# Order of the first loads, the norm of the input and the last root in a two-layer trunk on one core

## The chip, the cores and the metric

The kernel runs on one core of one Trainium2 chip. The metric is the device time of one execution in microseconds (us), the median of several runs. Engines are called by short names: PE is TensorE's matmul, PEld its weight load, DVE is VectorE, ACT is ScalarE, POOL is GpSimd, SP is SyncE, whose queue (SPq) issues nearly all loads.

## The reference, cut to what matters

Two layers over x, 256 tokens of 2048 features in float32. Layer 0 has a mixer of a convolution branch and an attention branch, layer 1 a gated recurrence; each mixer is followed by a gated feed-forward block. Ahead of each of the four blocks, and once at the end, stands this norm:

```
def rmsnorm(x, w):
    xf = x.astype(jnp.float32)
    y = xf * lax.rsqrt(jnp.mean(xf * xf, axis=-1, keepdims=True) + EPS)
    return (y * w.astype(jnp.float32)).astype(x.dtype)

h = rmsnorm(x, norm_w[layer, 0])
u = h @ w_in                       # layer 0: the first matmuls of the kernel
a, g = jnp.split(u[..., :2048], 2, axis=-1)
h = a * jax.nn.sigmoid(g)          # then the convolution over tokens
```

The last line of the trunk is `rmsnorm(x, final_norm_w)`.

## The kernel before, in words

**Precision.** Every large product is made from a high part and a low part of each factor (`fp32r`). `split` (L130) makes them for activations: ACT writes the high part (L138), DVE the low part (L139). `units` (L173) makes them for weights: it loads a raw tile (L184, three buffers), and for each unit of 128x1024 ACT writes the high part `whi` (L198) and DVE or POOL the low part `wlo` (L199; `lo_pool` says how many of four go to POOL). These two are traced with a raised priority (300).

**Norm by postponement.** The factor 1/rms of a token is not needed before a matmul. x goes in scaled by the norm's weight alone, and the product is multiplied by 1/rms afterwards, in the step that empties an accumulator. `norm_done` (L367) sums the squares, `inv_rms` (L152) takes the root (`rsqrt`, L141: a first guess from the bits and three rounds of three instructions), puts it on a diagonal (`rs_diag`, L162, two instructions) and broadcasts it with one matmul (L166); ACT copies the result to `rs_bc` (L168).

**The first layer's start.** x lies in memory twice, by features (`in_x`, for the matmuls) and by tokens (`in_xt`, for the squares). `run` (L1289) loads the small table `cst_a`, warms PE up with 12 products of ones (L1303), and `first_norm(i)` (L1308) loads a quarter of `in_x` in two halves and splits it. `even` (L422) then drives chunks of 256 columns of the input weights, one job each: 16 steps of 128 features, four units of four steps, 24 matmuls in a unit (L224 to L226), two accumulators. Chunk 0 is a gate chunk: `evac_g` multiplies the accumulator by `rs_bc` and takes the sigmoid; chunk 1 is its value chunk: `evac_a` multiplies it by that gate into `cin`, from which the convolution (L463 to L473, on DVE) starts. There are four accumulator banks (`ps_acc`), so two chunks can be in the making. In the text the units are numbered through: 0 to 3 are those of chunk 0 (each with a raw tile of its own, 512 KB), 4 to 7 those of chunk 1 (two raw tiles of 1 MB).

**What sets the order.** `drive` (L281) runs the jobs step by step and traces the background steps it is given between them, spread over the share `until` of the steps. A planner then orders each engine's instructions, by priority and by its own reckoning of when operands are there; on the chip each engine follows that order. In chunk 0 the background steps are the quarters 1 and 2 of x and `first_sums` (L1318), which takes quarter 3, the load of `in_xt` (2 MB), eight squares on ACT (L1326) and `norm_done`. In chunk 1 it is the load of the large table `cst_b` (838 KB).

**The end.** The last block's last column block is made one half of the tokens after the other (`half_job`, L261). `last` (L1342) adds the squares of each of four column blocks; with the last one it sums the four, takes the root with `rsqrt` and scales and stores the result. For the second half of the tokens this chain ends the kernel.

Of the kernel before, what the change touches and what calls it, by code (L numbers as in the profile page):

```python
# [10 lines left out]
F32 = mybir.dt.float32  # L11
F32R = mybir.dt.float32r
I32 = mybir.dt.int32
U8 = mybir.dt.uint8
AF = mybir.ActivationFunctionType
ALU = mybir.AluOpType
AX = mybir.AxisListType

S = 256
D = 2048  # L20
# [4 lines left out]
EPS = 1e-6  # L25
# [42 lines left out]
class Net:  # L68
# [58 lines left out]
    def quarter(self, tag, shape=(128, 4, 2, S), dtype=F32R):  # L127
        return self.tile(self.act, list(shape), tag, dtype, bufs=1)

    def split(self, dst, src, scale=None):  # L130

        nc = self.nc
        hi, lo = dst[:, 0, :], dst[:, 1, :]
        if scale is None:
            nc.scalar.activation(hi, src, AF.Copy)
            nc.vector.tensor_sub(lo, src, hi.bitcast(F32))
        else:
            nc.scalar.activation(hi, src, AF.Copy, scale=scale)  # L138
            nc.vector.scalar_tensor_tensor(lo, src, scale, hi.bitcast(F32), op0=ALU.mult, op1=ALU.subtract)  # L139
# [279 lines left out]

    def even(self, xhl, start):  # L422
        nc, a = self.nc, self.a
        ep_ctx, cv_ctx, ns_ctx = ExitStack(), ExitStack(), ExitStack()
        ep = self.ep = ep_ctx.enter_context(self.tc.tile_pool(name="ep", bufs=1))
# [9 lines left out]
        def scaled(ps):  # L435
            u = self.t256("e_u")
            nc.vector.tensor_mul(u, ps[:, :S], self.bc)
            return u

        def job(c, evac):  # L440
            return (8, self.w_job(wi[c], KD, xhl, evac, joint=True))

        def evac_g(i):
            def f(nt, ps):
                g = self.t256("f_g", bufs=4)
                nc.scalar.activation(g, scaled(ps), AF.Sigmoid)
                nc.gpsimd.tensor_mul(g, g, self.bc)
                gates[2 * i + nt] = g

            return f  # L450

        def evac_a(i):
            def f(nt, ps):
                j = 2 * i + nt
                nc.vector.tensor_mul(cin[:, j, PAD:], ps[:, :S], gates[j])

            return f
# [25 lines left out]
        def ln_steps():  # L483
            st = {}
            w, b = self.cb("lnw"), self.cb("lnb")
            four = lambda t: t.unsqueeze(1).to_broadcast([128, 4, S])

            def mean(j0, j1):
                if j0 == 0:
                    st["m"] = self.mx()[:, :S]  # L490
                for j in range(j0, j1):
                    nc.tensor.matmul(st["m"], self.mean1024, cy[:, j], start=(j == 0), stop=(j == 7))

            def center(h):
                y = cy[:, 4 * h : 4 * h + 4]
                nc.vector.tensor_sub(y, y, four(st["m"]))
                q = st[h] = self.quarter(f"mhl{h}", (128, 4, S), F32)
                nc.scalar.activation(q, y, AF.Square)

            def var():  # L500
                v = self.mx()[:, :S]
                for j in range(8):
                    nc.tensor.matmul(v, self.mean1024, st[j // 4][:, j % 4], start=(j == 0), stop=(j == 7))
                st["v"] = self.t256("rs_diag", bufs=1)
                nc.vector.tensor_scalar(st["v"], v, EPS, None, op0=ALU.add)
                st["r"] = self.t256("rs_bc", bufs=2)

            def root():
                self.rsqrt(st["r"], st["v"], "ln")

            def out(h):
                y = cy[:, 4 * h : 4 * h + 4]
                nc.vector.tensor_mul(y, y, four(st["r"]))
                for j in range(4 * h, 4 * h + 4):
                    nc.scalar.activation(cy[:, j], cy[:, j], AF.Silu, scale=w[:, j : j + 1], bias=b[:, j : j + 1])

            def parts(h):
                y = cy[:, 4 * h : 4 * h + 4]
                self.mhl(4 * h)
                q = self.mhl.have[h]  # L520
                nc.scalar.activation(q[:, :, 0, :], y, AF.Copy)
                nc.vector.tensor_sub(q[:, :, 1, :], y, q[:, :, 0, :].bitcast(F32))

            two = lambda f: [lambda: f(0), lambda: f(1)]
            rest = [self.rest]
            return [lambda: mean(0, 6)], (
                [lambda: mean(6, 8)] + two(center) + rest * 2 + [var, root] + two(out) + rest + two(parts)
            )
# [47 lines left out]
        def evac_c(kv):  # L576
# [9 lines left out]


        self.raw_size = 1024
        self.drive([job(0, evac_g(0))], start, until=0.75)
        self.raw_size = 2048  # L590
        self.lo_pool = (0, 1, 1, 1)
        ln_first, ln_rest = ln_steps()
        self.drive([job(1, evac_a(0))], [lambda: nc.sync.dma_start(self.cst_b, a["cst_b"])], until=0.25)
        self.drive(
            conv_job(1)
            + conv_job(2)
# [6 lines left out]
            until=0.98,  # L603
# [6 lines left out]
            until=0.8,  # L610
# [3 lines left out]
        sums = []  # L614
# [30 lines left out]
        for i in range(11):  # L645
            for late, k in ((3, "values"), (2, "turn0"), (2, "turn1"), (1, "weigh"), (0, "scores0"), (0, "scores1")):
                if 0 <= i - late < 8:
                    P, j = divmod(i - late, 4)
# [640 lines left out]
    def run(self):  # L1289
        nc, a = self.nc, self.a  # L1290
        self.cst_a = self.tile(self.fix, [128, NA], "cst_a")
        self.cst_b = self.tile(self.fix, [128, NB], "cst_b")
        nc.sync.dma_start(self.cst_a, a["cst_a"])
        self.x = self.tile(self.fix, [128, 2, D], "x")
        self.ones = self.tile(self.fix, [128, 128], "ones")
        nc.vector.memset(self.ones, 1.0)
        self.mean1024 = self.tile(self.fix, [128, 128], "mean1024")
        nc.vector.memset(self.mean1024, 1.0 / 1024)


        warm = self.mx()
        for _ in range(12):
            nc.tensor.matmul(warm[:, 0:128], self.ones, self.ones, start=True, stop=True)  # L1303

        xhl = self.new_xhl()
        xw = []

        def first_norm(i):  # L1308

            xw.append(self.quarter(f"mhl{i}", (128, 2, 4, S), F32))  # L1310
            for h in range(2):
                x = xw[i][:, 0, 2 * h : 2 * h + 2]
                nc.sync.dma_start(x, a["x"][:, i * 4 + 2 * h : i * 4 + 2 * h + 2, :])
            for j in range(4):
                f = 4 * i + j
                self.split(xhl(f), xw[i][:, 0, j], self.nw(0)[:, f : f + 1])

        def first_sums():  # L1318
            first_norm(3)
            nc.sync.dma_start(self.x, a["xt"])  # L1320
            self.ss = self.tile(self.tp, [128, 2, 4], "n_ss", bufs=2)
            with self.tc.high_priority(offset=-60):
                for tb in range(2):
                    for c in range(4):
                        junk = xw[c][:, 1].rearrange("p a b -> p (a b)")[:, tb * 512 : tb * 512 + 512]
                        nc.scalar.activation(  # L1326
                            junk, self.x[:, tb, c * 512 : c * 512 + 512], AF.Square, accum_out=self.ss[:, tb, c : c + 1]
                        )
            self.norm_done()

        first_norm(0)
        xhl = self.even(xhl, [lambda: first_norm(1), lambda: first_norm(2), first_sums])

        nxt = self.new_xhl()
        self.ffn(a["gu0"], a["dn0"], xhl, self.to_norm(self.nw(2), nxt))
        xhl = self.odd(nxt)

        fw = self.ctx.enter_context(self.tc.tile_pool(name="fw", bufs=1))
        fnw = self.tile(fw, [128, D], "fnw")
        nc.sync.dma_start(fnw, a["fnw"])  # L1340

        def last(c, tb):  # L1342

            self.square(c, tb)
            cols = [slice(i * 512, i * 512 + 512) for i in range(4)]
            x = [self.x[:, tb, i] for i in cols]
            if c < 3:
                nc.gpsimd.tensor_mul(x[c], x[c], fnw[:, cols[c]])
                return
            v = self.tile(self.tp, [128, 1], "l_v", bufs=2)  # L1350
            nc.vector.tensor_reduce(out=v, in_=self.ss[:, tb], op=ALU.add, axis=AX.X)
            nc.vector.tensor_scalar(v, v, 1.0 / D, EPS, op0=ALU.mult, op1=ALU.add)
            r = self.tile(self.tp, [128, 1], "l_r", bufs=2)
            self.rsqrt(r, v, "l")
            for i in (0, 1, 2, 3):
                if i == 3:
                    nc.vector.scalar_tensor_tensor(x[i], x[i], r, fnw[:, cols[i]], op0=ALU.mult, op1=ALU.mult)
                elif i == 0:
                    nc.vector.tensor_scalar(x[i], x[i], r, None, op0=ALU.mult)
                else:  # L1360
                    nc.scalar.activation(x[i], x[i], AF.Copy, scale=r)
                nc.sync.dma_start(a["out"][:, tb, cols[i]], x[i])

        self.ffn(a["gu1"], a["dn1"], xhl, last, keep=fw)


# [108 lines left out]
```

## Time and profile before

| | us |
|---|---|
| median of 3 runs | 2377.88 (2377.82 to 2378.31) |
| the profiled execution's own time | 2373.59 |
| span of its profile (first to last instruction) | 2371.8 |
| PE busy in it | 2350.5 |
| PE's mean granted clock | 0.997 of full |

The profile is that of one execution. Busy times don't tell how fast a matmul goes: PE counts as busy at either clock. The granted clock is given as a share of 2.4 GHz, so 0.50 is 1.2 GHz. In a row of a time line the first number is the start, the second the time from there to the end, both in us; "x4" merges four instructions; what stands in brackets is the engine's idle time just before and what ended it.

### The profile page before, as it was taken

To read this page: it belongs to the slowest core of one execution; us is meant where nothing else is said; L and a number is where in the kernel's file an instruction comes from. 1 tells how busy PE (TensorE), PEld (TensorE's weight loads), DVE (VectorE), ACT (ScalarE), POOL (GpSimd) and SP (SyncE) were. 2 spreads that over 40 slices of the span, in tenths; PEclk is the share of its full clock that TensorE was granted. 3 is DMA by queue.
4 is the path that set the end of the run, shared out by engine and by line. 5 is a ranking of instruction groups with operands and counts; after the bars stand their busy time and mean duration, and the time that the engine had idled before them with its cause. 6 is when DMAs were issued, how large, how long until landed. Compare 5 with 4: busy or idle time off the path is not lost.

```text
span 2371.8 us, 33574 instructions
## 1 busy us (share of the span) xinstructions
PE 2350.5 (99%) x13318; PEld 2026.6 (85%) x13318; DVE 1483.3 (63%) x2251; ACT 1144.2 (48%) x1648; POOL 401.7 (17%) x420
## 2 busy tenths in 40 slices
PE   8999999999999999999999999999999999999998
PEld 8999878888888888888888888888888888888886
DVE  5997677655555555555657777756555555555655
ACT  5345666554345434445544444445554344434443
POOL 4651311111011101110113333300110011101111
PEclk9999999999999999999999999999999999999999
DMA  7555534555555556555555445455555555555554
GB/s 254 188 167 168 179 108 145 193 184 189 195 193 182 185 188 198 191 182 182 194 171 180 167 149 178 143 196 187 185 194 186 191 192 187 187 195 194 181 179 157
DMA packets 62543, 430.82 MB, mean 182 GB/s; under 512 B 6961, under 2 KB 7089, under 8 KB 12209
## 3 DMA queue, kind: packets, MB, share of 16 engines
q1 hardware_dynamic: 62064, 428.15, 53.6%
q8 instruction: 104, 1.70, 0.3%
q10 hardware_dynamic: 320, 0.52, 0.1%
q14 instruction: 55, 0.44, 0.1%
HBM read 426.02 MB, written 2.10 MB: 181 GB/s over the span
## 4 chain that ended last, share of the span: by engine, by line
PE 97%; DVE 1%; DMA 1%; ACT 0%; POOL 0%; issue 0%; SPq 0%; ACTq 0%
PE acc L231 31%; PE acc L232 16%; PE acc L251 12%; PE acc L252 12%; PE acc L253 11%; PE acc L226 3%; PE acc L224 3%; PE acc L225 2%; PE acc L229 2%; PE acc L228 1%; PE mx L1127 1%; PE mx L711 1%; PE mx L816 0%; DMA x<-in_xt 0%; PE mx L337 0%; PE mx L893 0%
## 5 line engine op out<-in xcount | busy, mean ns | idle before, releaser
L199 DVE TENSOR_TENSOR wlo<-raw,whi 128x1024 fp32r<-128x1024 f32 x749 | 949.0, 1268 | 707.7 <-ACT whi L198 701.1
L198 ACT ACTIVATE whi<-raw 128x1024 fp32r<-128x1024 f32 x789 | 836.0, 1060 | 956.6 <-PE acc L253 404.3
L231 PE MATMUL acc<-xhl,whi 128*128 128x512 f32 x3120 | 1089.7, 395 | 0.0
L232 PE MATMUL acc<-xhl,wlo 128*128 128x256 f32 x3120 | 844.1, 280 | 0.0
L231 PEld LDWEIGHTS acc<-xhl,whi 128*128 128x128 f32 x3120 | 573.5, 188 | 113.8 <-issue 0.8
L232 PEld LDWEIGHTS acc<-xhl,wlo 128*128 128x128 f32 x3120 | 589.0, 189 | 24.7
L310 POOL TENSOR_TENSOR e_u<-e_s,rs_bc 128x256 f32<-128x256 f32 x192 | 150.2, 783 | 1468.0 <-DVE e_s L303 1240.1
L252 PE MATMUL acc<-wlo,mhl 128*128 128x512 f32 x932 | 363.7, 390 | 0.0
L253 PE MATMUL acc<-whi,mhl 128*128 128x512 f32 x932 | 363.5, 390 | 0.0
L251 PE MATMUL acc<-whi,mhl 128*128 128x512 f32 x932 | 338.8, 395 | 0.0
L251 PEld LDWEIGHTS acc<-whi,mhl 128*128 128x128 f32 x932 | 175.0, 188 | 40.4 <-issue 4.4
L253 PEld LDWEIGHTS acc<-whi,mhl 128*128 128x128 f32 x932 | 175.0, 188 | 36.5
L252 PEld LDWEIGHTS acc<-wlo,mhl 128*128 128x128 f32 x932 | 175.1, 188 | 34.8
L224 PE MATMUL acc<-xhl,whi 128*128 128x256 f32 (+1 forms) x528 | 149.6, 288 | 7.6 <-ACT whi L198 7.6
L301 ACT COPY e_c<-acc 128x256 f32<-128x256 f32 x208 | 77.5, 372 | 155.7 <-PE acc L229 155.6
L226 PE MATMUL acc<-xhl,wlo 128*128 128x256 f32 (+1 forms) x528 | 149.2, 287 | 0.6 <-DVE wlo L199 0.5
L225 PE MATMUL acc<-xhl,whi 128*128 128x256 f32 (+1 forms) x528 | 149.6, 286 | 0.0
L303 DVE TENSOR_TENSOR e_s<-acc,e_c 128x256 f32<-128x256 f32 x208 | 87.2, 421 | 68.7 <-ACT e_c L301 68.7
L252 PE MATMUL acc<-wlo,xhl 128*128 128x512 f32 x288 | 112.6, 391 | 0.0
L253 PE MATMUL acc<-whi,xhl 128*128 128x512 f32 x288 | 112.2, 390 | 0.0
L251 PE MATMUL acc<-whi,xhl 128*128 128x512 f32 x288 | 110.4, 396 | 0.0
L224 PEld LDWEIGHTS acc<-xhl,whi 128*128 128x128 f32 (+1 forms) x528 | 102.1, 193 | 8.3 <-ACT whi L198 8.1
(236 smaller groups left out, 1975.7 us busy)
## 6 DMA issues: line engine op xcount, KB each, us to landing
raw<-in_gu SPq DMA_DIRECT2D x176, 1024.0 KB, 5.0
raw<-in_dn SPq DMA_DIRECT2D x80, 1024.0 KB, 4.9
raw<-in_od_fq SPq DMA_DIRECT2D x32, 1024.0 KB, 5.1
raw<-in_od_ig SPq DMA_DIRECT2D x32, 1024.0 KB, 4.9
raw<-in_ev_in SPq DMA_DIRECT2D x30, 1024.0 KB, 5.0
raw<-in_ev_out SPq DMA_DIRECT2D x16, 1024.0 KB, 4.9
raw<-in_od_out SPq DMA_DIRECT2D x16, 1024.0 KB, 4.9
raw<-in_dn SPq DMA_DIRECT2D x16, 512.0 KB, 3.5
```

Of the source, the lines that this page charges most:

```text
L198: nc.scalar.activation(hi[:, :m], rs, AF.Copy)
L199: eng.tensor_sub(lo[:, :m], rs, hi[:, :m].bitcast(F32))
L224: nc.tensor.matmul(o[:, :S], h, a[:, 0, :], start=first, stop=False)
L225: nc.tensor.matmul(o[:, :S], h, a[:, 1, :], start=False, stop=False)
L226: nc.tensor.matmul(o[:, :S], l, a[:, 0, :], start=False, stop=end)
L231: nc.tensor.matmul(o, h, both, start=first, stop=False)
L232: nc.tensor.matmul(o[:, S:], l, a[:, 0, :], start=False, stop=False)
L251: nc.tensor.matmul(o, src(k)[:, 0, t], hi[:, i, :], start=(k == 0), stop=False)
L252: nc.tensor.matmul(o, src(k)[:, 0, t], lo[:, i, :], start=False, stop=False)
L253: nc.tensor.matmul(o, src(k)[:, 1, t], hi[:, i, :], start=False, stop=(k == nkt - 1))
L303: nc.vector.tensor_add(s, ps[:, :S], c)
L310: self.nc.gpsimd.tensor_mul(u, s, self.bc)
```

## The change

- Quarter 0 of x is split by DVE alone, high part and low part (`vector=True`).
- A copy of one column on ACT at the start, before anything else of ACT's.
- The load of `in_xt` goes from chunk 0's background into chunk 1's, pinned behind the loads traced before it on SP's queue (`keep_in_program_order`); so does that of `cst_b`, behind the weights of chunk 1's second half.
- The squares are taken under chunk 1, tokens 0 to 127 on ACT and 128 to 255 on DVE, two instructions of 128x1024 each; `norm_done` follows. Chunk 0's accumulators are held until then (`first_gates`, traced with a priority of 600).
- `lo_pool` is set behind chunk 1 instead of before it, so the low parts of units 4 to 6 are DVE's instead of POOL's.
- The last norm sums three of the four squares early, and its root works on −v/2, with two instructions in a round instead of three: 8 small instructions behind the last square instead of 12.

```
-    def split(self, dst, src, scale=None):
+    def split(self, dst, src, scale=None, vector=False):
         hi, lo = dst[:, 0, :], dst[:, 1, :]
+        if vector:
+            nc.vector.tensor_scalar(hi, src, scale, None, op0=ALU.mult)
+            nc.vector.scalar_tensor_tensor(lo, src, scale, hi.bitcast(F32), op0=ALU.mult, op1=ALU.subtract)
+            return
...
         self.raw_size = 1024
-        self.drive([job(0, evac_g(0))], start, until=0.75)
+        held = []
+        def first_gates():
+            with self.tc.high_priority(offset=600):
+                for nt, ps in held:
+                    evac_g(0)(nt, ps)
+        self.drive([job(0, lambda nt, ps: held.append((nt, ps)))], start, until=0.75)
         self.raw_size = 2048
+        ln_first, ln_rest = ln_steps()
+        sums = sums[:2] + [self.rest, lambda: self.tc.keep_in_program_order(nc.sync.dma_start(self.cst_b, a["cst_b"]))] + sums[2:]
+        self.drive([job(1, evac_a(0))], [self.rest] + sums + [first_gates], until=0.75)
         self.lo_pool = (0, 1, 1, 1)
-        ln_first, ln_rest = ln_steps()
-        self.drive([job(1, evac_a(0))], [lambda: nc.sync.dma_start(self.cst_b, a["cst_b"])], until=0.25)
...
+        nc.scalar.copy(self.tile(self.tp, [128, 1], "l_r", bufs=2), self.ones[:, 0:1])
         warm = self.mx()
...
-                self.split(xhl(f), xw[i][:, 0, j], self.nw(0)[:, f : f + 1])
+                self.split(xhl(f), xw[i][:, 0, j], self.nw(0)[:, f : f + 1], vector=i == 0)
-        def first_sums():
...
+        def first_squares(h):
+            if h == 0:
+                self.tc.keep_in_program_order(nc.sync.dma_start(self.x, a["xt"]))
+                self.ss = self.tile(self.tp, [128, 2, 2], "n_ss1", bufs=1)
+            for tb in range(2):
+                junk = xw[2 * h + tb][:, 1].rearrange("p a b -> p (a b)")
+                x = self.x[:, tb, h * 1024 : h * 1024 + 1024]
+                out = self.ss[:, tb, h : h + 1]
+                if tb == 0:
+                    nc.scalar.activation(junk, x, AF.Square, accum_out=out)
+                else:
+                    nc.vector.tensor_tensor_reduce(
+                        out=junk, in0=x, in1=x, scale=1.0, scalar=0.0, op0=ALU.mult, op1=ALU.add, accum_out=out
+                    )
-        xhl = self.even(xhl, [lambda: first_norm(1), lambda: first_norm(2), first_sums])
+        xhl = self.even(
+            xhl,
+            [lambda i=i: first_norm(i) for i in (1, 2, 3)],
+            [lambda: first_squares(0), lambda: first_squares(1), self.norm_done],
+        )
...
+                if c == 2:
+                    p = part[tb] = self.tile(self.tp, [128, 1], "l_p", bufs=2)
+                    nc.vector.tensor_reduce(out=p, in_=self.ss[:, tb, 0:3], op=ALU.add, axis=AX.X)
+                    nc.vector.tensor_scalar(p, p, EPS * D, None, op0=ALU.add)
                 return
-            self.rsqrt(r, v, "l")
+            nc.vector.tensor_scalar(h, self.ss[:, tb, 3:4], part[tb], -0.5 / D, op0=ALU.add, op1=ALU.mult)
+            nc.vector.tensor_scalar(r.bitcast(I32), h.bitcast(I32), -0.5, 519526879.0, op0=ALU.mult, op1=ALU.add)
+            for _ in range(3):
+                nc.vector.scalar_tensor_tensor(q, r, h, r, op0=ALU.mult, op1=ALU.mult)
+                nc.vector.scalar_tensor_tensor(r, q, 1.5, r, op0=ALU.add, op1=ALU.mult)
```

## Rows read from the trace of the kernel before

**Rows 1.** The page, busy time of each engine.
```profile
PE 2350.5 (99%) x13318; PEld 2026.6 (85%) x13318; DVE 1483.3 (63%) x2251; ACT 1144.2 (48%) x1648; POOL 401.7 (17%) x420
```

**Rows 2.** The time line of PE: start, time, instruction, idle before and its releaser.
```profile
8.99 0.38 PE L224 MATMUL acc<-xhl,whi 128*128 128x256 f32 x1 [2.45 <-ACT whi L198]
...
10.25 0.39 PE L226 MATMUL acc<-xhl,wlo 128*128 128x256 f32 x1 [0.52 <-DVE wlo L199]
...
19.87 0.28 PE L226 MATMUL acc<-xhl,wlo 128*128 128x256 f32 x1
25.27 0.58 PE L224 MATMUL acc<-xhl,whi 128*128 128x256 f32 x1 [5.12 <-ACT whi L198]
...
27.76 0.41 PE L225 MATMUL acc<-xhl,whi 128*128 128x256 f32 x1
27.97 0.41 PE L226 MATMUL acc<-xhl,wlo 128*128 128x256 f32 x1
...
32.62 0.70 PE L166 MATMUL mx<-rs_diag,ones 128*128 128x256 f32 x2 [0.95 <-DVE rs_diag L162]
...
44.06 0.28 PE L226 MATMUL acc<-xhl,wlo 128*128 128x256 f32 x1
```

**Rows 3.** Table by stage: stretch, length, busy (instructions), PEclk, DMA share, GB/s.
```profile
10.40:14.00 3.60, 3.60 (x19) 3.60 (x20) 3.60 (x8) 3.60 (x8) 0.00 (x0) 0.53 1.11 446
14.00:20.20 6.20, 6.15 (x51) 5.94 (x50) 3.21 (x7) 2.62 (x8) 0.00 (x0) 1.00 0.97 411
25.30:31.00 5.70, 5.66 (x25) 5.37 (x26) 5.46 (x10) 2.02 (x3) 3.23 (x2) 0.50 0.75 270
33.00:44.20 11.20, 11.20 (x95) 11.17 (x94) 3.01 (x5) 5.48 (x7) 7.28 (x5) 1.00 0.58 189
```

**Rows 4.** The time line of ACT.
```profile
4.99 1.28 ACT L138 ACT_TABLE_LOAD   x1 [4.99 <-DMA mhl<-in_x]
...
7.89 1.04 ACT L198 ACTIVATE whi<-raw 128x1024 fp32r<-128x1024 f32 x1
...
19.23 0.63 ACT L1326 ACTIVATE mhl<-x 128x512 f32<-128x512 f32 x1 [3.58 <-DMA x<-in_xt]
...
24.16 1.06 ACT L198 ACTIVATE whi<-raw 128x1024 fp32r<-128x1024 f32 x1
```

**Rows 5.** Weights of units 0 and 3: issue on SP's queue; size and us to landing.
```profile
2.12 0.43 SPq L184 DMA_DIRECT2D raw<-in_ev_in  x1
...
raw<-in_ev_in SPq DMA_DIRECT2D x1, 512.0 KB, 5.5
...
10.42 0.33 SPq L184 DMA_DIRECT2D raw<-in_ev_in  x1
...
raw<-in_ev_in SPq DMA_DIRECT2D x1, 512.0 KB, 13.6
```

**Rows 6.** Groups of DVE by line and shape: count, busy us, mean ns, idle before.
```profile
L139 DVE SCALAR_TENSOR_TENSOR xhl<-mhl,cst_a,xhl 128x256 fp32r<-128x256 f32 x16 | 6.7, 478 | 5.6 <-ACT xhl L138 5.6
...
L827 DVE CUSTOM_DVE_ANT_0 a_z<-mx,cst_b 128x256 f32<-128x256 f32 x32 | 11.8, 419 | 4.6 <-PE mx L816 4.6
L827 DVE CUSTOM_DVE_ANT_0 a_z<-mx,cst_b 128x128 f32<-128x128 f32 x32 | 7.3, 283 | 0.7 <-PE mx L816 0.7
...
L162 DVE TENSOR_SCALAR rs_diag<-cst_a,rs_tok 128x128 f32<-128x128 f32 x8 | 6.3, 824 | 0.1
```

**Rows 7.** Time lines of DVE and POOL around the broadcast of the norm.
```profile
25.25 1.22 DVE L199 TENSOR_TENSOR wlo<-raw,whi 128x1024 fp32r<-128x1024 f32 x1
...
27.75 4.81 DVE L162 TENSOR_SCALAR rs_diag<-cst_a,rs_tok 128x128 f32<-128x128 f32 x2
...
27.77 7.05 POOL L199 TENSOR_TENSOR wlo<-raw,whi 128x1024 fp32r<-128x1024 f32 x3 [25.07 <-ACT whi L198]
```

**Rows 8.** The time line of DVE at the end: first and last of twelve.
```profile
2363.43 0.16 DVE L1351 TENSOR_REDUCE l_v<-n_ss 128x1 f32<-128x4 f32 x1 [0.85 <-ACT n_sq L325]
...
2365.55 0.16 DVE L150 SCALAR_TENSOR_TENSOR l_r<-lq,l_r 128x1 f32<-128x1 f32 x1
```

More of the change, by code (lines that the diff above doesn't have):

```diff
@@ L418, in ffn, with even @@
             self.drive(jobs)
-    def even(self, xhl, start):
+    def even(self, xhl, start, sums):
         nc, a = self.nc, self.a
@@ L1315, in first_norm @@
                 f = 4 * i + j
-                self.split(xhl(f), xw[i][:, 0, j], self.nw(0)[:, f : f + 1])
-        def first_sums():
[L1319 to L1329, printed above, removed]
-        first_norm(0)
-        xhl = self.even(xhl, [lambda: first_norm(1), lambda: first_norm(2), first_sums])
+                self.split(xhl(f), xw[i][:, 0, j], self.nw(0)[:, f : f + 1], vector=i == 0)
[13 more added lines that the diff above has]
+                    )
+        first_norm(0)
+        xhl = self.even(
[3 more added lines that the diff above has]
+        )
         nxt = self.new_xhl()
@@ L1340, in run @@
         nc.sync.dma_start(fnw, a["fnw"])
+        part = [None, None]
         def last(c, tb):
@@ L1348, in last @@
                 nc.gpsimd.tensor_mul(x[c], x[c], fnw[:, cols[c]])
+                if c == 2:
+                    p = part[tb] = self.tile(self.tp, [128, 1], "l_p", bufs=2)
+                    nc.vector.tensor_reduce(out=p, in_=self.ss[:, tb, 0:3], op=ALU.add, axis=AX.X)
+                    nc.vector.tensor_scalar(p, p, EPS * D, None, op0=ALU.add)
                 return
-            v = self.tile(self.tp, [128, 1], "l_v", bufs=2)
-            nc.vector.tensor_reduce(out=v, in_=self.ss[:, tb], op=ALU.add, axis=AX.X)
-            nc.vector.tensor_scalar(v, v, 1.0 / D, EPS, op0=ALU.mult, op1=ALU.add)
+            h = self.tile(self.tp, [128, 1], "l_v", bufs=2)
+            nc.vector.tensor_scalar(h, self.ss[:, tb, 3:4], part[tb], -0.5 / D, op0=ALU.add, op1=ALU.mult)
             r = self.tile(self.tp, [128, 1], "l_r", bufs=2)
-            self.rsqrt(r, v, "l")
+            nc.vector.tensor_scalar(r.bitcast(I32), h.bitcast(I32), -0.5, 519526879.0, op0=ALU.mult, op1=ALU.add)
+            q = self.tile(self.tp, [128, 1], "l_q", bufs=2)
+            for _ in range(3):
+                nc.vector.scalar_tensor_tensor(q, r, h, r, op0=ALU.mult, op1=ALU.mult)
+                nc.vector.scalar_tensor_tensor(r, q, 1.5, r, op0=ALU.add, op1=ALU.mult)
             for i in (0, 1, 2, 3):
```

## The prediction

> **What bounds the kernel now.** I began with the busy shares: PE is busy for 2350.5 us of the 2371.8 us span [rows 1]. So the change can only win where PE stands still or runs at its lower clock, and it touches two such places, the first 45 us and the last 10.
>
> PE's own time line shows the start [rows 2]. Chunk 0's first matmul starts at 8.99, after 2.45 us idle; the low part of the first weights costs 0.52 more; unit 2 ends at about 20.0, and unit 3 starts only at 25.27, after 5.12 us idle. The two matmuls near 28 us stand 0.21 us apart. The broadcast of the norm (L166) starts at 32.62 after 0.95 idle, with everything behind it on PE waiting. Chunk 1's last matmul starts at 44.06.
>
> The table by stage gives the clock [rows 3]. From 33.0 to 44.2 it is 1.00 (2.4 GHz) and 95 matmuls take 11.2 us, so 0.12 each. From 25.3 to 31.0, right after the 5.12 us idle, it is 0.50 (1.2 GHz). An earlier fall (0.53 from 10.4 to 14.0) follows the 2.45 us idle.
>
> The time line of ACT shows who was late [rows 4]. It idles 3.58 us for x in rows (in_xt), squares it in eight pieces from 19.23 on, and takes the high part of unit 3 only at 24.16. But the squares are not the whole cause: unit 3's weights were issued at 10.42 and landed 13.6 us later, at 24.0 [rows 5], queued behind in_xt and cst_b. Moving the squares alone would win almost nothing; the order of the loads is what matters.
>
> **The change part by part.** The sum is made against the profiled execution, 2373.6 us (span 2371.8); the median of the runs is 2377.9, 4.3 above it, and I carry the difference over to that.
>
> *Start.* ACT loses its table load (1.28 us at 4.99) to an earlier point, where it waits only for a memset, and four scaled copies. Unit 0's high part began at 7.89 [rows 4]; now it waits only for its weights, issued at 2.12 and landing 5.5 later, at 7.62 [rows 5]. Gain 0.26. DVE gets eight parts instead of four: at 0.48 each [rows 6] (the four new ones have one tensor operand, so 0.48 is an upper bound) 3.8 us from 4.99, done at 8.8, when the high part ends too: no cost. The PE idle before stays near 2.2 us, so I leave the first clock fall as it is.
>
> *Loads of unit 3.* in_xt (2.10 MB) and cst_b (0.86 MB) no longer stand ahead of them. At 411 GB/s [rows 3] they took 7.2 us, so unit 3's weights land near 16.8; high part (1.06) until 17.9, low part (1.22) until 19.1 [rows 4, 7], needed at 19.7. The 5.28 us from 19.99 to 25.27 go. With them goes the clock fall behind: from 25.3 to 31.0 the pitch was 0.21 instead of 0.12, so 43% of 5.7 us is lost: 2.5. Beside it: the Trainium skill (TensorE: Matmul & The Clock Gate, Terms) prices such time at its length times (1 − K/N), here one half, 2.9 us, and by that the sum would be 9.7 instead of 9.3. The row decides: a full-clock matmul takes 0.12, more than half of 0.21.
>
> *Squares under chunk 1.* Next in the same queue: 1 MB for units 4 and 5 (2.55 us at 411 GB/s: 19.4), in_xt (5.1: 24.5), 1 MB for units 6 and 7 (27.0), cst_b (29.1). PE at 0.12 a matmul, 24 in a unit, 2.88, starts unit 4 at 22.6, unit 5 at 25.5, unit 6 at 28.4. ACT squares half of the data in two pieces; all of it in eight took 4.93 (19.23 to 24.16), so 2.5: 24.5 to 27.0 [rows 4]. DVE's fused form is bounded by L827, 0.283 us for 128 columns and 0.419 for 256 [rows 6], so 1.06 ns per further column, 1.24 for 1024 and, with the accumulator, 1.3; twice makes 2.6, to 27.1. Unit 6's high part runs 27.0 to 28.1, its low part on DVE 28.1 to 29.3. PE can start on the high part, so it waits between 0 (low part at once) and 2.3 us (norm chain first on DVE). I take 0.7, nearer the low end since the weights' parts are traced with a higher priority than the squares.
>
> *Norm and L166.* Before, the two diag instructions took 4.81 us while POOL worked on low parts [rows 7]; all eight of the run mean 0.824 [rows 6], so the six others mean (6.6 − 4.8)/6 = 0.3. Three low parts of chunk 1 go from POOL (7.05/3 = 2.35 each) to DVE (1.22) [rows 7], so POOL is still and the diag takes 0.6. The chain is 12 small instructions (0.19 each: 2.3) plus the diag from 27.1, with unit 6's low part in between: 31.2. L166 then fits under unit 7: the 0.95 us that PE waited for it [rows 2] go; at worst they stay. DVE's load in chunk 1 is 4.9 + 2.6 + 2.9 + 0.8 = 11.2 us of some 12.5: covered, but closely.
>
> *Held accumulators.* Chunk 0's two banks are emptied only after the broadcast, near 32.5; chunk 2 wants them at 35. cst_b, moved past one load of weights and the norm's input, lands at 29.1, first wanted by the convolution after chunk 1; chunk 2's first weights land at 31.7. All three are covered by chunk 1 itself.
>
> *Tail.* From 2363.43 to 2365.71, 12 small DVE instructions run in a chain at 0.193 us each [rows 8]. Eight remain: 0.77 us off the end. The two new sums at the third column block run while DVE waits for PE.
>
> Sum: 0.26 + 5.28 + 2.5 + 0.95 − 0.7 + 0.77 = 9.06, and 0.2 for the slow restart at 25.27 (that matmul took 0.58, those after it 0.41) [rows 2]: 9.3. So 2373.6 − 9.3 = 2364.3 under the profiler, and 2377.9 − 9.3 = **2368.6** as the median. Behind chunk 1 I change nothing: PE never waits for more than about a microsecond there in the profile, and all engines shift together. A measurement of this kernel can tell some 0.2%, 4.8 us, from no change.
>
> **Rivals.**
> *1. Squares queued ahead of unit 5's parts.* The written order of ACT and DVE is fixed before the run, and before the squares did stand ahead of unit 3's high part. Then ACT idles until 24.5, unit 5's high part ends at 28.1 instead of being ready at 25.5: 2.6 us of waiting, and perhaps the lower clock behind it (up to 2.5). Gain 4.1 to 6.7, about 2372.5. Against: unit 5's weights land five microseconds ahead of in_xt.
> *2. Ahead of unit 4's too.* Then PE waits 5.5 us at 22.6, as long as before, with the clock fall behind it: 8.0 lost, gain 1.3, 2376.6. That is also how it looks if the change merely moves the wait.
> *3. Late weights for unit 6.* They stand behind in_xt. At the 270 GB/s of the stage from 25.3 to 31.0 [rows 3] the 4.19 MB behind unit 3's take 15.5 us and land at 32.3; PE waits 5.0, plus 2.5 of clock; less the 0.7 taken, the gain is 2.5, 2375.4. Against: that stage was limited by free buffers, not by the queue; for: unit 3's 13.6 us [rows 5] show that what is issued later lands later. The Trainium skill (DMA: Bandwidth & Descriptors, Queues, rings and completion order) says that each DMA engine takes descriptors in the order of its ring, which speaks against putting 2 MB ahead of weights; by that rule the trace agrees, since unit 3's weights came in behind the two large loads.
> *4. Slower: chunk 2 waits for held banks.* If the norm chain on DVE stands behind later units' work, the two banks stay full and PE stops at chunk 2's first matmul. It decides from a chain end later than 34.4 on, one for one: for 4.8 us slower than before it must end at about 48.5, 17 later than worked out. Price for that: 2382.7. For: four banks in all, two held. Against: the chain's priority and 3 us of margin.
>
> **How the numbers follow.** Forecast 0.70; rival 1 0.17; rival 2 0.05; rival 3 0.05; rival 4 0.03. The range: below, the first clock fall vanishes too (1.5), no wait at unit 6 (0.7) and 0.5 of restart losses: gain 12.0, so 2365.9, and I say 2365.5. Above, all of rival 1 (2373.8, said as 2374.0); rivals 2 to 4, 0.13 together, are left out. Faster by over 0.2%: the forecast and three quarters of rival 1, 0.83; within: the rest of rival 1, rivals 2 and 3, 0.14; slower 0.03.
>
> **What would show it.** In the profile after: unit 0's high part starting near 7.7; no idle near 20 us; granted clock 1.00 from 14 us on; the squares of 128x1024 on ACT and DVE starting between 23 and 25; the diag at 0.3 each; chunk 1's last matmul near 35 instead of 44; and 8 instructions in the last chain. An idle of several us of PE with "whi" or "wlo" as releaser between 22 and 31 us is rival 1, 2 or 3 (told apart by whether ACT is squaring or idle for DMA); PE waiting at 35 for chunk 0's banks is rival 4. I am wrong if chunk 1 ends early and the span still doesn't shrink: then something behind it has turned into a wait.

## The result, and the profile after

| | before | after |
|---|---|---|
| median of 6 runs each | 2378.10 (2377.22 to 2378.71) | 2365.36 (2364.69 to 2366.11) |
| profiled execution, its own time | 2373.59 | 2365.47 |
| span of its profile | 2371.8 | 2363.7 |

The ratio is 0.995, with a 95% interval of 0.9938 to 0.9962: 12.7 us faster (9.0 to 14.7 by that interval), where 9.3 were forecast. Between the two profiles there are only 8.1 us. The median and the profiled execution of the kernel before are 4.5 us apart, those of the changed kernel 0.1. That gap turned out to be the most instructive thing in this case.

The time line of PE after the change, the same lines of code as in [rows 2] (four lines further down in the file):

```profile
9.66 0.58 PE L228 MATMUL acc<-xhl,whi 128*128 128x256 f32 x1 [3.85 <-ACT whi L202]
...
33.62 0.59 PE L170 MATMUL mx<-rs_diag,ones 128*128 128x256 f32 x2
```

PE starts later than before, and from then on waits for nothing in the first 60 us: the 5.12 us at 25.27 and the wait for the broadcast are gone. The table by stage answers to [rows 3]:

```profile
10.40:14.00 3.60, 3.56 (x17) 3.27 (x16) 3.60 (x8) 3.60 (x9) 0.00 (x0) 0.50 1.04 408
14.00:20.20 6.20, 6.20 (x50) 6.20 (x49) 5.21 (x10) 4.55 (x7) 0.00 (x0) 0.91 0.99 372
20.20:25.30 5.10, 5.10 (x45) 5.10 (x44) 2.60 (x3) 1.39 (x2) 0.00 (x0) 1.00 1.00 419
25.30:31.00 5.70, 5.70 (x50) 5.70 (x49) 5.39 (x14) 3.87 (x6) 0.00 (x0) 1.00 1.02 427
```

From 25.3 to 31.0 the clock is 1.00 instead of 0.50, and 50 matmuls run where 25 did. The first fall of the clock stayed, behind 3.85 us of idle PE. ACT, against [rows 4]:

```profile
8.55 1.06 ACT L202 ACTIVATE whi<-raw 128x1024 fp32r<-128x1024 f32 x1 [6.34 <-DMA raw<-in_ev_in]
...
16.43 1.06 ACT L202 ACTIVATE whi<-raw 128x1024 fp32r<-128x1024 f32 x1
...
24.97 1.06 ACT L1342 ACTIVATE mhl<-x 128x1024 f32<-128x1024 f32 x1 [2.81 <-DMA x<-in_xt]
...
27.53 2.01 ACT L202 ACTIVATE whi<-raw 128x1024 fp32r<-128x1024 f32 x2 [0.37 <-DMA raw<-in_ev_in]
```

Unit 3's high part starts at 16.43 instead of 24.16; the squares wait for in_xt until 24.97 (24.5 was worked out), unit 6's high part starts at 27.53 (27.0). Unit 3's weights, against [rows 5], landed 5.4 us after their issue instead of 13.6. The issue on SP's queue:

```profile
10.90 0.33 SPq L188 DMA_DIRECT2D raw<-in_ev_in  x1
```

and, among the DMA issues of that moment (KB and us from issue to landing):

```profile
raw<-in_ev_in SPq DMA_DIRECT2D x1, 512.0 KB, 5.4
```

DVE around the broadcast, against [rows 7]:

```profile
31.87 0.48 DVE L166 TENSOR_SCALAR rs_diag<-cst_a,rs_tok 128x128 f32<-128x128 f32 x2
34.66 0.76 DVE L441 TENSOR_TENSOR e_u<-acc,rs_bc 128x256 f32<-128x256 f32 x2 [2.30 <-ACT rs_bc L172]
```

and POOL's time line:

```profile
33.20 4.77 POOL L203 TENSOR_TENSOR wlo<-raw,whi 128x1024 fp32r<-128x1024 f32 x2 [30.50 <-ACT whi L202]
```

The diag takes 0.48 us instead of 4.81. It ends 0.85 us before POOL begins. At the end, against [rows 8], first and last two of eight instead of twelve:

```profile
2355.79 0.21 DVE L1379 TENSOR_SCALAR l_v<-n_ss,l_p 128x1 f32<-128x1 f32 x1 [0.85 <-ACT n_sq L329]
...
2357.12 0.22 DVE L1384 SCALAR_TENSOR_TENSOR l_q<-l_r,l_v 128x1 f32<-128x1 f32 x1
2357.37 0.16 DVE L1385 SCALAR_TENSOR_TENSOR l_r<-l_q,l_r 128x1 f32<-128x1 f32 x1
```

1.74 us instead of 2.28. Eight at the old 0.193 each would be 1.54; but three of the eight take 0.22 and one 0.21, where the twelve took 0.15 to 0.16.

### The profile page after: what moved, and what is told of

Read it like the earlier page. It is cut to its first block, busy times and chain, and to the rows that moved or that the text cites. A ratio compares the mean times of both kernels' runs of the same rounds, so it can differ in the third digit from the quotient of the medians.

```text
span 2363.7 us, 33564 instructions
## 1 busy us (share of the span) xinstructions
PE 2348.0 (99%) x13318; PEld 2025.9 (86%) x13318; DVE 1485.7 (63%) x2258; ACT 1140.4 (48%) x1633; POOL 395.5 (17%) x417
## 4 chain that ended last, share of the span: by engine, by line
PE 98%; DVE 0%; DMA 0%; ACT 0%; POOL 0%; issue 0%; SPq 0%; ACTq 0%
PE acc L235 31%; PE acc L236 16%; PE acc L255 12%; PE acc L257 12%; PE acc L256 12%; PE acc L228 3%; PE acc L230 3%; PE acc L229 3%; PE acc L233 2%; PE acc L232 1%; PE mx L1140 1%; PE mx L724 1%; PE mx L829 0%; PE mx L341 0%; PE mx L906 0%; PE mx L1231 0%
```

## The experiments

All medians below are to be held against 2365.4 for the changed kernel; the kernel before, which ran beside every group of experiments, had medians of 2377.6 to 2378.0.

**The kernel before, once more (no edit).**

> The kernel before, unchanged. Its one profile shown so far was that of an execution of 2373.6 us, while the median of its six runs is 2378.1; the changed kernel's runs all lie within 2364.7 to 2366.1. Theory: the usual execution of the kernel before differs from the profiled one in the first 45 us alone, by later landings and a longer time at the lower clock: PE's last matmul of chunk 1 starts near 48.5 us instead of 44.1, and everything behind it is shifted by 4 to 5 us. Rival: the difference is spread over the whole run; then chunk 1 ends at 44 to 45 us again while the span is 4 us longer.

Ten runs: four from 2373.5 to 2374.0, six from 2377.1 to 2378.4. The profile fell on one of 2377.7 us. PE in it:

```profile
9.36 0.58 PE L224 MATMUL acc<-xhl,whi 128*128 128x256 f32 x1 [3.32 <-ACT whi L198]
...
25.75 0.52 PE L224 MATMUL acc<-xhl,whi 128*128 128x256 f32 x1 [4.54 <-ACT whi L198]
...
35.22 0.70 PE L166 MATMUL mx<-rs_diag,ones 128*128 128x256 f32 x2 [4.09 <-DVE rs_diag L162]
```

DVE, the norm chain of chunk 0:

```profile
27.06 2.35 DVE L148 TENSOR_TENSOR rsq<-rs_tok 128x2 f32<-128x2 f32 x1
29.45 2.32 DVE L149 SCALAR_TENSOR_TENSOR rsq<-rsq,rs_v 128x2 f32<-128x2 f32 x1
31.80 2.26 DVE L150 SCALAR_TENSOR_TENSOR rs_tok<-rsq,rs_tok 128x2 f32<-128x2 f32 x1
34.10 0.16 DVE L148 TENSOR_TENSOR rsq<-rs_tok 128x2 f32<-128x2 f32 x1
```

POOL:

```profile
27.02 7.02 POOL L199 TENSOR_TENSOR wlo<-raw,whi 128x1024 fp32r<-128x1024 f32 x3 [24.32 <-ACT whi L198]
```

and the table by stage behind the broadcast:

```profile
33.00:44.20 11.20, 8.98 (x61) 8.93 (x62) 4.00 (x9) 4.50 (x6) 2.89 (x4) 0.85 0.33 102
```

POOL makes three low parts of 2.34 us from 27.02 on. Each time, one instruction of two columns on DVE, 0.16 us at 34.10, lasts as long as POOL's. In the profile of [rows 7] POOL began at 27.77, when the small instructions were through, and met only the two of the diag. So the two profiled executions differ in how many instructions of the norm chain meet POOL, three or two, and PE's wait for the broadcast is 4.09 or 0.95 us. Behind the longer wait the clock falls too: from 33.0 to 44.2 it is 0.85, with 61 matmuls (2.2 us of the wait lie in that stretch), instead of 1.00 with 95 in [rows 3]. The whole difference of the two spans, 4.1 us, is there when DVE first empties an accumulator of chunk 1 into `cin` (47.10 against 43.01 us), as the theory had it. That most of it is POOL, and the landings only some 0.5 us (unit 3 starts at 25.75 instead of 25.27), was not in it.

**Low parts of units 4 to 6 on DVE, nothing else changed.**

```
-        self.lo_pool = (0, 1, 1, 1)
         ln_first, ln_rest = ln_steps()
         self.drive([job(1, evac_a(0))], [lambda: nc.sync.dma_start(self.cst_b, a["cst_b"])], until=0.25)
+        self.lo_pool = (0, 1, 1, 1)
```

> The kernel before with one thing changed: the low parts of units 4 to 6 are made by DVE instead of POOL (lo_pool set behind chunk 1). In the usual execution of the kernel before (2377.7 us in the profile) three small DVE instructions of the norm chain took 2.3 us each beside POOL's three low parts of 2.35 us and L166 made PE wait 4.1 us; in the one of 2373.6 us only the two diag instructions did, and it waited 0.95 us. Theory (POOL's low parts hold up the DVE instructions that run beside them): no small DVE instruction over 0.3 us around 27 us, PE's wait for L166 under 1 us, the time 3.5 to 5 us below the kernel before, and all its runs within 2 us of each other instead of two groups 4 us apart. Rival (the low parts only move from one engine to the other, and DVE now delays the chain by their 1.2 us each): the wait for L166 stays above 2 us, the time within 1.5 us of the kernel before.

2372.6 us, ratio 0.9981 (0.9972 to 0.9991), all ten runs between 2371.5 and 2373.7. In its time line of DVE:

```profile
27.10 0.16 DVE L148 TENSOR_TENSOR rsq<-rs_tok 128x2 f32<-128x2 f32 x1
27.30 0.16 DVE L149 SCALAR_TENSOR_TENSOR rsq<-rsq,rs_v 128x2 f32<-128x2 f32 x1
...
29.46 1.22 DVE L199 TENSOR_TENSOR wlo<-raw,whi 128x1024 fp32r<-128x1024 f32 x1
30.59 0.15 DVE L149 SCALAR_TENSOR_TENSOR rsq<-rsq,rs_v 128x2 f32<-128x2 f32 x1
30.78 0.16 DVE L150 SCALAR_TENSOR_TENSOR rs_tok<-rsq,rs_tok 128x2 f32<-128x2 f32 x1
30.98 0.48 DVE L162 TENSOR_SCALAR rs_diag<-cst_a,rs_tok 128x128 f32<-128x128 f32 x2
```

and in PE's, without idle time before it:

```profile
33.83 0.59 PE L166 MATMUL mx<-rs_diag,ones 128*128 128x256 f32 x2
```

The chain has three low parts of 1.22 us in it, where the kernel before has one, and still ends at 31.5 instead of 35.2; PE doesn't wait for the broadcast. One moved line is worth 4.9 us against the 2377.6 beside it, more than the 4.09 of waiting, as the lower clock behind it goes too; and the two groups are gone. Against the lower group of the kernel before (about 2373.6) it is 1.0 us, the size of the 0.95 that PE waited there. The rival falls.

**The loads early, all else as changed.**

```
-                self.tc.keep_in_program_order(nc.sync.dma_start(self.x, a["xt"]))
...
-            [lambda i=i: first_norm(i) for i in (1, 2, 3)],
+            [lambda: first_norm(1), lambda: first_norm(2), lambda: (first_norm(3), nc.sync.dma_start(self.x, a["xt"]))],
...
-        sums = sums[:2] + [self.rest, lambda: self.tc.keep_in_program_order(nc.sync.dma_start(self.cst_b, a["cst_b"]))] + sums[2:]
+        sums = sums[:2] + [self.rest, lambda: nc.sync.dma_start(self.cst_b, a["cst_b"])] + sums[2:]
```

> The changed kernel, with the loads of in_xt and cst_b issued as early as before, ahead of the weights of unit 3; squares still on ACT and DVE under chunk 1, short root kept. Theory (the order of the loads is the cause): the weights of unit 3 land near 24 us again, PE idles 4 to 6 us at 20 us with the lower clock behind it, and the time is 7 to 9 us above the changed kernel's 2365.4. Rival (the eight squares on ACT ahead of the weights' high part are the cause): no idle of PE over 1 us at 20 us, the time within 2 us of the changed kernel's.

2372.0 us (2371.2 to 2373.0, ten runs), ratio 0.9977 (0.9967 to 0.9986): 6.7 above the changed kernel. PE's time line has the old wait:

```profile
25.07 0.58 PE L228 MATMUL acc<-xhl,whi 128*128 128x256 f32 x1 [4.91 <-ACT whi L202]
```

ACT's, at the same place:

```profile
23.96 1.06 ACT L202 ACTIVATE whi<-raw 128x1024 fp32r<-128x1024 f32 x1 [2.72 <-DMA raw<-in_ev_in]
```

and the table by stage, behind the wait:

```profile
25.30:31.00 5.70, 5.66 (x25) 5.37 (x26) 3.89 (x6) 2.21 (x3) 0.00 (x0) 0.50 0.78 267
```

The clock there is 0.50, as in [rows 3]. ACT is free, idles 2.72 us, and the weights still come only at 23.96: the order of the loads is the cause, and where the squares stand is not. This kernel and the one before it share short norm chains without POOL and differ by 0.6 us, which the tail (0.55 us, below) would cover.

**All squares on ACT, in eight pieces, under chunk 1.**

```
-                    nc.scalar.activation(junk, x, AF.Square, accum_out=out)
-                else:
-                    nc.vector.tensor_tensor_reduce(
...
+                for c in (2 * h, 2 * h + 1):
+                    junk = xw[c][:, 1].rearrange("p a b -> p (a b)")[:, tb * 512 : tb * 512 + 512]
+                    nc.scalar.activation(
+                        junk, self.x[:, tb, c * 512 : c * 512 + 512], AF.Square, accum_out=self.ss[:, tb, c : c + 1]
+                    )
```

> The changed kernel with all squares on ACT in eight pieces, as before the change, but still under chunk 1 and behind the weights' loads. Theory: the squares end at about 29.9 instead of 27.2 us and hold up the high parts of units 6 and 7 by 2.4 us where the planner puts them first; PE then waits 1 to 2.5 us at unit 6 and the norm is 2.5 us later: 1 to 3 us longer than the changed kernel. Rival (the place of the squares matters, not the engine): within 0.5 us of the changed kernel.

2368.4 us: 3.0 longer. PE's time line shows the wait that was expected, in two parts:

```profile
31.21 0.38 PE L228 MATMUL acc<-xhl,whi 128*128 128x256 f32 x1 [1.69 <-ACT whi L202]
...
32.47 0.58 PE L230 MATMUL acc<-xhl,wlo 128*128 128x256 f32 x1 [0.52 <-DVE wlo L203]
```

ACT's shows where it comes from:

```profile
30.12 1.99 ACT L202 ACTIVATE whi<-raw 128x1024 fp32r<-128x1024 f32 x2
```

Unit 6's high part starts at 30.12 instead of 27.53, behind the eight squares. Behind PE's wait its clock falls as well, to 0.65 from 33.0 to 37.0, where the changed kernel has 1.00. Once the loads are in order, the split of the squares between ACT and DVE, with larger pieces, is worth 3 us.

**POOL's share back under chunk 1**, measured twice.

```
+        self.lo_pool = (0, 1, 1, 1)
         self.drive([job(1, evac_a(0))], [self.rest] + sums + [first_gates], until=0.75)
-        self.lo_pool = (0, 1, 1, 1)
```

> The changed kernel with lo_pool set ahead of chunk 1 as before, so that POOL makes the low parts of units 4 to 6. Theory: only unit 6's low part (near 28.6 us) runs beside the norm chain, so one or two of its instructions take 2.3 us, the diag is 2 to 4 us later than in the changed kernel, L170 makes PE wait 0 to 2.5 us and the time is 0 to 2.5 us longer. Rival (DVE is the tight engine under chunk 1): relief on DVE makes it 0.5 to 1 us shorter.

2372.7 us, where at most 2.5 more than 2365.4 was expected: two runs of 2365.8 and 2366.3, four of 2372.3 to 2374.0. Its profile is of the 2365.8. DVE there:

```profile
32.27 0.48 DVE L166 TENSOR_SCALAR rs_diag<-cst_a,rs_tok 128x128 f32<-128x128 f32 x2
```

and POOL:

```profile
32.52 4.86 POOL L203 TENSOR_TENSOR wlo<-raw,whi 128x1024 fp32r<-128x1024 f32 x2 [2.14 <-ACT whi L202]
```

One small instruction of the chain was held (2.22 us from 28.18 on), but the diag began 0.25 us before POOL's low parts for chunk 2, and its two instructions took 0.24 each.

> The changed kernel with POOL making the low parts of units 4 to 6, once more, for its second profile: its runs fell into two groups, 2365.8 to 2366.3 and 2372.3 to 2374.0, and the profile shown was of the first, with one small DVE instruction of the norm chain held for 2.2 us. Theory (where an execution falls depends on how many of the chain's instructions meet POOL's low parts): a profile of the second group has two or more DVE instructions of 2.2 us or more between 24 and 36 us, a later broadcast, and PE waiting 3 us or more for it or for the banks held until then. Rival (the groups come from the loads or the clock): the DVE chain looks the same and the wait stands elsewhere.

Eight runs, median 2369.9: four from 2365.5 to 2367.3, four from 2372.5 to 2373.1. This time the profile was of the upper group (2373.1). PE:

```profile
30.93 0.39 PE L230 MATMUL acc<-xhl,wlo 128*128 128x256 f32 x1 [1.70 <-POOL wlo L203]
37.84 1.22 PE L170 MATMUL mx<-rs_diag,ones 128*128 128x256 f32 x2 [4.25 <-DVE rs_diag L166]
```

DVE:

```profile
28.61 2.28 DVE L154 SCALAR_TENSOR_TENSOR rs_tok<-rsq,rs_tok 128x2 f32<-128x2 f32 x1
...
33.15 4.64 DVE L166 TENSOR_SCALAR rs_diag<-cst_a,rs_tok 128x128 f32<-128x128 f32 x2
```

POOL:

```profile
28.52 2.35 POOL L203 TENSOR_TENSOR wlo<-raw,whi 128x1024 fp32r<-128x1024 f32 x1 [3.23 <-PE acc L230]
33.05 4.65 POOL L203 TENSOR_TENSOR wlo<-raw,whi 128x1024 fp32r<-128x1024 f32 x2 [2.17 <-ACT whi L202]
```

and the table by stage:

```profile
33.00:44.20 11.20, 6.95 (x37) 6.57 (x37) 6.91 (x9) 4.01 (x6) 6.08 (x4) 0.70 0.57 191
```

Unit 6's low part holds one instruction for 2.28 us, as expected. That pushes the diag to 33.15, 0.1 us behind the start of POOL's low parts for chunk 2, and both its instructions are held for 2.3 us each. The first meeting brings the chain so close to POOL's next work that some 0.35 us decide on a second one. The expectation had counted the first alone, and it had no lower clock behind the wait: 0.70 from 33.0 to 44.2. The rival of the second expectation falls, since the DVE chain differs.

**in_xt behind both halves of chunk 1's weights.**

```
+        late = lambda: (sums[0](), self.tc.keep_in_program_order(nc.sync.dma_start(self.cst_b, a["cst_b"])), sums[1]())
-        self.drive([job(1, evac_a(0))], [self.rest] + sums + [first_gates], until=0.75)
+        self.drive([job(1, evac_a(0))], [self.rest] * 6 + [late, sums[2], first_gates], until=0.75)
```

> The changed kernel with the load of in_xt behind both halves of chunk 1's weights instead of between them (cst_b behind it). Theory: unit 6's weights land 5 us earlier, which gains nothing since PE doesn't wait there at its first clock fall; in_xt lands 2.5 us later, at 27.5 instead of 25.0, and the broadcast near 36.5 instead of 34.3. Chunk 0's two banks were emptied at 35.4 in the changed kernel and chunk 2 starts at 35.8, so now PE waits about 2 us for the broadcast or the held banks: 1.5 to 3 us longer than the changed kernel's 2365.4. Rival (the norm has slack under chunk 1, the weights of unit 6 have none): within 0.5 us of it or up to 1 us shorter.

2371.5 us: three runs of 2365.0 to 2366.1, one of 2368.5, six of 2371.4 to 2372.2. The profile is of an execution of 2371.8 us. PE:

```profile
37.98 0.70 PE L170 MATMUL mx<-rs_diag,ones 128*128 128x256 f32 x2 [3.12 <-DVE rs_diag L166]
39.60 0.58 PE L228 MATMUL acc<-xhl,whi 128*128 128x256 f32 x1 [0.92 <-DVE e_u L441]
```

DVE:

```profile
33.01 2.36 DVE L154 SCALAR_TENSOR_TENSOR rs_tok<-rsq,rs_tok 128x2 f32<-128x2 f32 x1
35.41 2.52 DVE L166 TENSOR_SCALAR rs_diag<-cst_a,rs_tok 128x128 f32<-128x128 f32 x2
```

POOL:

```profile
32.96 4.68 POOL L203 TENSOR_TENSOR wlo<-raw,whi 128x1024 fp32r<-128x1024 f32 x2 [30.26 <-ACT whi L202]
```

The chain is late enough to meet POOL's low parts for chunk 2 twice. The broadcast is late, and then PE waits 0.92 us for chunk 0's banks, rival 4 of the prediction in small. The runs at 2365 suggest that the norm had slack for the late load itself, as the rival said, and that the loss is the meeting with the lower clock behind it (0.75 from 33.0 to 44.2); none of those runs was profiled. The loss is larger than the 1.5 to 3 us expected.

**The old start** (no early copy; quarter 0 split by ACT and DVE).

```
-        nc.scalar.copy(self.tile(self.tp, [128, 1], "l_r", bufs=2), self.ones[:, 0:1])
...
-                self.split(xhl(f), xw[i][:, 0, j], self.nw(0)[:, f : f + 1], vector=i == 0)
+                self.split(xhl(f), xw[i][:, 0, j], self.nw(0)[:, f : f + 1])
```

> The changed kernel without the early copy on ACT and with quarter 0 split by ACT and DVE as before. In three profiles of the changed start, ACT waits idle 5 to 6 us for unit 0's weights, and PE starts 1.1 us after they land, as it does with the old start in the usual execution of the kernel before (weights 8.25, PE 9.36). Theory: the start is worth nothing beyond 0.3 us, time within 0.5 us of the changed kernel. Rival: the table load and the four copies of ACT delay the first high part by 0.3 us or more, and with it the whole: 0.3 to 1 us longer.

2365.3 us, the changed kernel's time. ACT takes unit 0's high part at 7.46 in its profile, right behind its copies; with the changed start it idles until the weights land, between 7.2 and 8.5 us in the profiles here.

**The old root at the end.**

```
-                if c == 2:
...
-            nc.vector.tensor_scalar(h, self.ss[:, tb, 3:4], part[tb], -0.5 / D, op0=ALU.add, op1=ALU.mult)
...
+            self.rsqrt(r, v, "l")
```

> The changed kernel with the old root in the last norm (12 small instructions behind the last square instead of 8). The profile of the changed kernel shows 1.74 us for the 8 against 2.31 for the 12, so the theory expects the chain 0.5 to 0.6 us longer and the time 0.6 us longer, which the timing of whole runs can hardly tell; the prediction had 0.77. Rival: nothing, since the last store is waited for in any case; then the time from the last matmul to the end stays the same.

2365.7 us, too close to 2365.4 to tell by whole runs. From PE's last matmul (start 2353.27) to the end of the span (2363.7) the profile has 10.4 us, against 9.9 in the changed kernel (2353.82 to 2363.7): 0.55 us for four instructions.

**More products of ones: 19 instead of 12.**

```
-        for _ in range(12):
+        for _ in range(19):
```

> The changed kernel with 19 products of ones at the start instead of 12. In the changed kernel PE ends them at 5.8 us, idles 3.85 us until the first weights and then works at half clock from 8.5 to 15 us. Theory: with PE busy until about 8.6 us the granted clock stays at 1.00 through the first 20 us, which is worth 5.5 us x 0.43 = 2.4 us, less up to 1.1 us of new waiting for the weights of unit 6: 1.3 to 2.4 us faster than the changed kernel. Rival: the loads set the pace of the first 30 us, so the faster clock is given back as waits and the time stays within 0.5 us.

2364.8 us, 0.55 below the changed kernel, less than can be told. In its profile the clock is 1.00 throughout, and PE gives the time back:

```profile
8.76 0.39 PE L228 MATMUL acc<-xhl,whi 128*128 128x256 f32 x1 [1.56 <-ACT whi L202]
10.02 0.39 PE L230 MATMUL acc<-xhl,wlo 128*128 128x256 f32 x1 [0.52 <-DVE wlo L203]
27.68 0.39 PE L228 MATMUL acc<-xhl,whi 128*128 128x256 f32 x1 [0.60 <-ACT whi L202]
29.06 0.38 PE L230 MATMUL acc<-xhl,wlo 128*128 128x256 f32 x1 [0.65 <-DVE wlo L203]
```

At full clock PE reaches unit 6 before its high and low part are there (0.60 and 0.65 us). The rival is nearer: in the first 30 us the loads set the pace.

**POOL's share one chunk later still**, alone and with 19 products.

```
-        self.lo_pool = (0, 1, 1, 1)
+        on = [lambda: setattr(self, "lo_pool", (0, 1, 1, 1))]
...
-            conv[:-20] + ln_first + conv[-20:],
+            conv[:11] + on + conv[11:-20] + ln_first + conv[-20:],
```

> The changed kernel with POOL's share of the low parts beginning one chunk later, so that the three low parts that POOL made from 33.2 us on are DVE's too. In the changed kernel the diag ends at 32.35 us, 0.85 us before POOL's first low part. Theory: nothing is gained in the usual execution, since nothing meets there; the time is within 0.7 us of 2365.4 and no execution lies over 2367. Rival (DVE, which starts the convolution at 39 us, falls behind with 3.7 us more work): 0.5 to 2 us longer.

2365.2 us, five runs from 2364.6 to 2365.5: the theory held; DVE has room for the three low parts.

> The same with 19 products of ones at the start. With 19 alone the clock stayed at 1.00, the time was 2364.8 and one of four runs was 2368.3. Theory: that one run was a meeting of the norm chain with POOL; without it all runs lie within 1.5 us of each other around 2364.3 to 2365.0, 0.4 to 1 us below the changed kernel. Rival: the outlier comes from the loads, so it is there again, and the median is that of the changed kernel.

2365.4 us (2365.1 to 2365.8). The outlier of 2368.3 didn't come back in five runs, which is too few to put it down to POOL, and nothing was gained: in this profile the products of ones ended at 6.9 us, PE idled 1.48 us, and the clock from 10.4 to 14.0 was 0.54 after all. With 19 alone 1.56 us of idle had left it at 1.00, so the length of that idle alone doesn't tell. No version here beats the changed kernel by more than can be measured.

## Why the prediction was right or wrong

It was right in direction and about the loads, its largest term, and low by 3.4 us of gain. The median, 2365.36, lies 0.14 below the lower end of its range. Against the profile, for which the sum was made, it was 1.2 us too hopeful (2365.47 for 2364.3): PE starts 0.67 us later instead of 0.26 earlier, the tail brings 0.22 less, 0.7 taken for unit 6 did not come, and about 0.7 of what is missing isn't accounted for.

- **The order of the loads: right.** 7.8 us, less 0.7 for a new wait, were worked out for the wait at 25.27 and the lower clock behind it; putting the loads back costs 6.7. The landings came within 0.5 us of those worked out (16.3 for 16.8, 25.0 for 24.5, 27.4 for 27.0).
- **The step that failed: "I carry the difference over".** The 4.3 us between the profiled execution and the median were taken as a constant. They were the same fault as a term of the sum, in its larger size: POOL holding up the norm chain. In the sum it has 0.95 us, from a profile in which the chain met POOL twice; in the usual execution it met POOL three times and PE waited 4.09. Taking POOL away from the kernel before gives 4.9 us, the lower clock behind the wait included. With that in place of 0.95, the sum is 9.3 + 3.9 = 13.2, against 12.7 measured. The parts as measured one by one, 6.7 for the loads, 4.9 for POOL and 0.55 for the tail, make 12.2; 0.5 us isn't assigned.
- **The start: wrong.** 0.26 us were expected, and whole runs show nothing (2365.3 with the old start). The weights' landing at 7.62 was read from one execution; in the others it lies between 7.2 and 8.5, and PE starts 1.1 us behind the start of the high part with either start.
- **The first clock fall** was left as it was. In the profile after it is longer (0.50 from 10.4 to 14.0 and still 0.91 behind), with 3.85 us of idle PE ahead of it instead of 2.45. It cost less than its length: where the clock stayed up, PE waited 1.25 us at unit 6.
- **The wait at unit 6:** 0.7 taken; none in the profile after, 0.18 to 0.90 in those of the old tail and the old start, 1.25 in the one where the clock stayed up. Rival 3 was never seen beyond that.
- **The tail:** 0.77 expected, 0.55 measured. The four small instructions that take their scalar by pointer last 0.21 to 0.22 us, the four without 0.15 to 0.16, in steps of 0.25 to 0.26 and of 0.18 to 0.19; the prediction had 0.193 a step for all.
- **Rivals 1 and 2** did not come: the squares stand behind units 4 and 5. With eight squares on ACT they came in small, at unit 6 (1.69 and 0.52 us of waiting). The lower of rival 1's two gains is 9.3 − 5.1 = 4.2, not 4.1.
- **Rival 4** was seen where in_xt was later still; it was set off by POOL, which it didn't name. The margin of 3 us that was given for the norm chain is 0.85 us against POOL's first low part.

## What to carry to other kernels

When a kernel's profiled execution and its median disagree, don't carry the difference over: profile a second execution and look for a wait that differs. Here its length depended on which of two engines began first, and a change that removed it won more than the first profile showed. On a queue that is full, put the loads in the order of need, and count what stands ahead of a late one before blaming the engine that waits. A chain of tiny DVE instructions that ends a wait should not run beside POOL work on SBUF: here that cost 4.9 us.

## What the runs showed of the hardware that was not expected

A DVE instruction of two columns (0.16 us) lasted 2.22 to 2.36 us when POOL had begun a `TENSOR_TENSOR` of some 2.35 us just before it. Where POOL started its next one at once, a chain of dependent small instructions on DVE got through one per POOL instruction: 27.06, 29.45, 31.80 us. DVE instructions with one input in PSUM ran at their usual speed beside POOL (`e_u`, 0.76 us for two at 34.66, while POOL was busy from 33.20 to 37.97; also 0.76 at 36.36 in the kernel before, with POOL still). The Trainium skill (SBUF — State Buffer, Who interferes with whom) states this rule: DVE and POOL share a pair of ports, and a DVE instruction with two SBUF inputs, or in a two-port mode, is blocked for the whole length of a POOL instruction that reads SBUF and started first. The trace agrees for the small instructions and for `e_u`; the diag has one tensor input and was held too, which would be the two-port case, but no row names the mode. With the rule the prediction could have priced each meeting; how many there are in an execution only the second profile told.

Weights of 512 KB issued at 2.1 us landed between 5.1 and 6.4 us later from one execution to the next. The fall of PE's clock in the first 15 us varies too, but not in step with it: after landings of 5.5 us the clock from 10.4 to 14.0 was 0.50, 0.56 and 0.76 in three executions (in_xt late, POOL's share first and again). The times vary little: the six runs of the changed kernel lie within 1.4 us.
